# A fp32 decoder block on one core: low parts of the split weights first, one product split a tick later, and token roots spread through DRAM

## The chip, the cores and the metric

The kernel runs on one core of one Trainium2 chip. The metric is the device time of one execution in microseconds, lower is better; the figure of a kernel is the median of its runs.

## The reference, cut to what matters

One layer on 2048 tokens of width 1024, everything in float32:

```python
h = rms_norm(x, norm_g)                       # one root per token
u = h @ w_in                                  # 9728 columns: conv v, B, C, z; q, k, v, attn z; two gates
y_c = b_c * causal_depthwise_conv(c_c * v_c, conv_w) * silu(z_c)
y_a = y_c @ w_conv_out
q, k = rms_norm(q, q_norm_g), rms_norm(k, k_norm_g)
o = sliding_window_attention(q, k, v, sinks) * silu(z_a)   # window 128, blocks of 128, 16 heads on 4 kv heads
y_b = o @ w_attn_out
merged = g_a * y_a + g_b * y_b                # sigmoid gates
x + merged @ w_out
```

Almost all of the arithmetic is matrix products with 1024 on the contracted side.

## The kernel before

**Tiles and products.** The 2048 tokens are worked in two tiles of 1024 (`T`), each in two halves of 512 (`H`). A product of weights and activations is made from three TensorE passes: each operand is rounded to a "high" part by a copy on ScalarE (ACT), and the rest, the "low" part, is left by a subtraction on VectorE (DVE); TensorE (PE) then adds high·high, high·low and low·high. `product` (L467) issues these as 12 matmuls of 128x512: for each of four chunks two with the high weights and a third with the low ones.

**Units.** A unit is a block of 256 output columns for one tile. `sunit` (L486) computes it in a Strassen-like form with seven products in place of eight, in the order 1, 5, 6, 2, 7, 3, 4, on three PSUM banks called X, V and Y. Its weights come as pieces (`pieces_of`, L361): piece "a" (for products 1, 2), "d" (product 4), "sums" (additions and subtractions on the raw weights, four DVE steps of 128x512), then "s" (products 6 and 5) and "t" (products 3 and 7). Each of a, s and t is a high part of 128x1024 on ACT and a low part of 128x1024 on DVE; the names in the profile end in `_ah`/`_al`, `_sh`/`_sl`, `_th`/`_tl`. A ring of weight slots lets the s piece of the next unit be made only once product 3 of this one is through, so it has two products' time until product 5 of the next unit reads it.

**Ticks.** The order of the work is written by hand. `run` (L668) steps through the products; one step is a tick, some 2.7 us of TensorE. In each tick it issues, in this order: the product with what ends it (`fin`), the high part of one weight piece (`hi`), the first three functions that were put on this tick (`at`, filled by `put`), the low part (`lo`), the other functions, and four steps of the woven chains. `Woven` (L208) holds chains of small DVE steps, and slips one of them in behind each DVE instruction. Every engine works through its own instructions in the order in which they were issued; engines wait for each other by semaphores.

**What ends a product.** For the q units `fin_q` (L793) copies or adds the result to `qt`, splits it (`parts`, L832: `q_h` on ACT, `q_l` on DVE) and writes both to DRAM. For product 7 the result is a pair (Y, s5), which DVE adds; the ACT part waits for that add, and the DVE part for the ACT one. For the last z units (`za`), `fin_z` (L1192) multiplies by SiLU and hands the chunk to `use_y` (L1743), which, for the last two chunks, at once forms operands from it (`ca`, `form`: again a copy on ACT and a subtraction on DVE, `ophc` in the profile).

**Token roots.** RMSNorm's root of each token is computed with the tokens on the partitions (`rt`, `rtok`, four columns for a half). The activations are used with the tokens along the free axis, so the roots have to be spread over all partitions: `x_roots` (L598) makes four TensorE transposes of 128x128 into a PSUM bank (`ptr`), and one ACT copy to `rb`. For the first tile `turned` (L1513) does it on ticks 6 and 12 (`TURNED_AT`), while the k and v products run; for the second tile `roots` in `next_tile` (L1671) does it on ticks 9 and 17 of the first tile's last stage (`ya`, L1230), and `norm_l` (from tick 11) and `norm_r` (from tick 18) multiply by `rb` on DVE (`h<-h,cols,rb`). In the stage `ya` the SP queue carries the loads of gate values (`tha`, L1328) and weights.

Of the kernel before, what the change touches and what calls it, by code (L numbers as in the profile page):

```python
# [58 lines left out]
K_AT = (1, 1, 4)  # L59

T0_SHIFT = 1
TURNED_AT = (6, 12)

K_ROOT = True
CSUM_AT = (5, 8, 11, 14)
CONV_AT = (2, 2, 3, 3, 4, 4, 5, 5, 6, 6, 7, 7, 8, 8, 9, 9, 10, 10, 11, 11, 12, 12, 13, 13, 15, 15, 16, 16, 18, 18, 19, 19)
WO_AT = (29, 29, 30, 30, 31, 31, 32, 32)
# [24 lines left out]
def block_kernel(  # L92
# [51 lines left out]

    vd = dram.tile([NKV, HD, S // HD + 2, P], F32, name="vd")
    krd = [dram.tile([2, 2, T], F32, name=f"krd{t}") for t in range(NT)]
    od = [dram.tile([KC, P, T], F32, name=f"od{t}") for t in range(NT)]
    ocd = [dram.tile([KC, P, T], F32, name=f"ocd{t}") for t in range(NT)]
    yd = [dram.tile([KC, P, T], F32, name=f"yd{t}") for t in range(NT)]
# [4 lines left out]
    def hs(q):  # L154
        return slice(q * H, (q + 1) * H)
# [124 lines left out]
    def sub(o, a, b, eng=None):  # L280
        return (eng or vec).tensor_tensor(out=o, in0=a, in1=b, op=ALU.subtract)
# [23 lines left out]
    def added(n):  # L305

        if n not in summed_in:
            summed_in.add(n)
            raw = raws[2 * n + 1]
            if by_dma(plan[n][2]):  # L310
                nc.gpsimd.dma_start(raw[:, 0, 1], block_of(n, 1, 1), accum_op=ALU.add)
            else:
                return (lambda: add(raw[:, 0, 1], raw[:, 0, 1], raw[:, 1, 1]),)
        return ()
# [46 lines left out]
    def pieces_of(n):  # L361

        kind, srcs, key = plan[n]
        name = "w" + "_".join(str(i) for i in key)
        w = {}

        def two(hi, lo, src):
            return (lambda: nc.scalar.copy(hi, src),  # L370
                    lambda: vec.tensor_tensor(
                        out=lo, in0=src, in1=hi.bitcast(F32), op=ALU.subtract))

        if kind == "R":
            return w, []

        if kind in "SP":
            def pair(h, m1, m2, nm):
                hi, lo = (v.rearrange("p (i j c) -> p i j c", i=2, c=P) for v in wpair(f"{name}_{nm}"))
                for i, m in enumerate((m1, m2)):  # L380
                    w[m] = (hi[:, i], lo[:, i])
                raw = raws[2 * n]
                return two(hi, lo, raw[:, h] if summed else raw[:, :, h])

            summed = []

            if kind == "P":
                return w, [(2, 2 * h, lambda h=h: pair(h, (h, 0), (h, 1), f"p{h}")) for h in range(2)]

            def single():  # L390
                hl = wpool.tile([P, 2, KP, P], F32R, tag="w", name=f"{name}_d")
                w[4] = (hl[:, 0], hl[:, 1])
                return two(hl[:, 0], hl[:, 1], raws[2 * n + 1][:, 1, 1])

            def sums():
                raw = raws[2 * n]

                def f():
                    summed.append(vec.chain(
                        *added(n),  # L400
                        lambda: sub(raw[:, 0, 0], raw[:, 0, 1], raw[:, 0, 0]),
                        lambda: sub(raw[:, 1, 1], raw[:, 1, 1], raw[:, 0, 0]),
                        lambda: sub(raw[:, 1, 0], raw[:, 1, 0], raw[:, 0, 0])))

                return (lambda: None, f)

            def of_sums(*args):
                summed[0]()
                return pair(*args)

            return w, [(2, 0, lambda: pair(0, 1, 2, "a")), (1, 0, single), (0, 0, sums),
                       (2, 0, lambda: of_sums(0, 6, 5, "s")), (2, 2, lambda: of_sums(1, 3, 7, "t"))]

        def part(p):
            hi, lo = (v.rearrange("p (j c) -> p j c", c=UC) for v in wpair(f"{name}_{p}"))
            w[p] = (hi, lo)
            return two(hi, lo, raws[2 * n + p])

        return w, [(2, 0, lambda: part(0)), (2, 2, lambda: part(1))]
# [10 lines left out]
    def piece():  # L430

        if not todo and (len(ready) > used[0] or not open_prep()):
            return None
        n, i, cost, last, f = todo[0]
        need = [2 * n + i] if plan[n][0] in "TP" else [2 * n, 2 * n + 1][: 1 + min(i, 1)]
        if live[0] + cost > WRING or any(k not in raws for k in need):
            return None
        todo.pop(0)
        live[0] += cost
        rawlive[0] -= last  # L440
        return f()

    def force(n, m):

        while m not in ready[n]:
            ab = piece()
            assert ab is not None, (plan[n], m, live)
            for f in ab:
                f()

    def unit(key):
# [146 lines left out]
    def x_roots(t, q, rs):  # L598

        pt = mbank(f"ptr{t}_{q}")  # L600
        for b in range(HB):
            nc.tensor.transpose(pt[:, b, :], rs[:, b : b + 1].to_broadcast([P, P]), ident)
        rb = slot([P, H], F32, f"rb{t}_{q}")
        nc.scalar.copy(rb, pt.rearrange("p b q -> p (b q)"))
        return rb

    def gain(c):
        return cols[:, C_G + c : C_G + c + 1]

# [59 lines left out]
    def run(gen):  # L669
        while True:  # L670
            tick[0] += 1
            if next(gen, gen) is gen:
                tick[0] -= 1
                return
            ahead_loads()
            hi, lo = (piece() if tick[0] >= W_FROM else None) or (None, None)
            if hi:
                hi()

            fs = at.pop(tick[0], [])  # L680
            for f in fs[:3]:
                f()
            if lo:
                lo()
            for f in fs[3:]:
                f()
            vec.some(WOVEN)

# [10 lines left out]
    class KV:  # L699
# [20 lines left out]

        def values(self, n):
            rooted[n // 2]()
            for b in (2 * n, 2 * n + 1):
                v = slot([P, NKV, 2, HD], F32R, f"v0_{b}")
                src = self.banks[b][:, UC:].rearrange("p (j d) -> p j d", d=HD)
                r = rtok[:, b : b + 1]
                nc.scalar.activation(out=v[:, :, 0], in_=src, func=AF.Copy, scale=r)
                vec.scalar_tensor_tensor(
                    out=v[:, :, 1], in0=src, scalar=r, in1=v[:, :, 0].bitcast(F32),
                    op0=ALU.mult, op1=ALU.subtract)  # L730
                for e, half in enumerate(HALVES):
                    nc.gpsimd.dma_start(
                        vd[:, :, 2 * (b + 1) + e].rearrange("j k d -> k j d"),
                        v[half].bitcast(F32).rearrange("p j l d -> p j (l d)"))
# [58 lines left out]
    def fin_q(t, j):  # L793
# [4 lines left out]
        def fin(i, q, val):  # L798
            nm = f"q{t}_{j}_{i}_{q}"
            qt = slot([P, H], F32, f"{nm}_t")  # L800
            into(qt, val)

            wait = QWAIT if (t, j) == (0, 0) else 0
            if wait:
                put(tick[0] + wait, lambda: parts(i, q, qt))
            else:
                parts(i, q, qt)

            def sums():
                if by_pe:  # L810
                    pt = turn4(qt, f"pt{nm}")
                else:
                    pt = mbank(f"pt{nm}")
                    vec.transpose(out=pt.rearrange("p b q -> p (b q)"), in_=qt)
                sq = head_square(pt, nm)
                put(tick[0] + 1, lambda: reduce(sq))

            def reduce(sq):
                if by_pe:
                    head_reduce(sq, ss, 2 * i + q)  # L820
                else:
                    n = 2 * i + q
                    vec.tensor_reduce(
                        out=ss[:, n * 16 : (n + 1) * 16], in_=sq.rearrange("p (h d) -> p h d", d=32),
                        axis=AX.X, op=ALU.add)
                left[0] -= 1
                if left[0] == 0:
                    put(tick[0] + 1, rms)

            put(tick[0] + 1 + (wait if by_pe else TURN_WAIT), sums)  # L830
# [820 lines left out]
    def next_tile(t, n0):  # L1651
# [19 lines left out]
        def roots(q):  # L1671
            for b0 in (q * HB, q * HB + 2):
                seen_[b0]()
            st.setdefault("rb", {})[q] = x_roots(t, q, rt[q])

        rt, seen_ = {}, {}
        for b, n in enumerate((0, 1, 1, 2, 3, 4, 5, 6)):
# [3 lines left out]
        for g, n in enumerate((5, 6, 10, 11)):  # L1681
            put(n0 + n, lambda g=g: norm(2 * g))
            put(n0 + n + 1, lambda g=g: seen_[2 * g]())
        for q, n in enumerate((9, 17)):
            put(n0 + n, lambda q=q: roots(q))
        for c in range(KC):
            put(n0 + 6 + c // 2, lambda c=c: raw_load(t, 0, c, st))
# [18 lines left out]
    for t in range(NT):  # L1706
# [36 lines left out]
        def use_y(k, q, y):  # L1743
            att["raw"][k, q] = y
            if k >= KC - 2:
                ca(B_AT[k % 2, q], k // 2)

        zs = [("z", j) + fin_z(t, j, yd[t], "z", use_o) for j in range(NJ)]
        zs += [("za", j) + fin_z(t, j, od[t], "za", use_y) for j in range(NJ)]
# [141 lines left out]
```

## Time and profile before

| | |
|---|---|
| median of 3 runs | 1916.77 us (1916.73 to 1917.03) |
| the profiled execution | 1917.32 us, of which the profiled span is 1915.6 us |
| TensorE busy | 1904.0 us, 99% of the span, at full granted clock |
| VectorE busy | 1539.6 us, 80% |
| ScalarE busy | 991.7 us, 52% |
| GpSimd busy | 594.3 us, 31% |

How to read it: an instruction is named by its line, engine, operation and "out<-in" by the program's tiles. A row of waits has the engine that waited, then what it waited for, the total in microseconds, how many times, and the longest. In rows in order of time the first two numbers are the start and the duration in microseconds, and a note in brackets gives the idle time of the engine before the row and what ended it. A matmul of 128x512 is shown with 0.39 us though the next one starts 0.23 us after it, since matmuls overlap in the pipeline; so idle time that is shown for TensorE is smaller than what a wait costs.

### The profile page before, as it was taken

The page shows a single profiled execution, that of the slowest core. Times are in us where ns is not written, and L with a number is a line of the kernel's source. Part 1 is how long each engine was busy: PE and PEld are TensorE (multiplying, and loading weights), DVE is VectorE, ACT ScalarE, POOL GpSimd, SP SyncE. Part 2 cuts the span into 40 slices and gives each one's busy share as a digit, 9 for nine tenths or more (in the row PEclk, how much of TensorE's full clock was granted, in tenths as well). Part 3 has the DMA queues.
Part 4 walks back from the last instruction along what each step waited for, and adds up shares of the span by engine and source line. Part 5 has one row for each costly group of instructions (what it writes and reads, how often), then busy time and mean ns, then how long its engine had stood idle before and what let it go on. Part 6 is the DMA issues. An engine that isn't in the chain of part 4 may idle for free.

```text
span 1915.6 us, 27253 instructions
## 1 busy us (share of the span) xinstructions
PE 1904.0 (99%) x8718; PEld 1581.2 (83%) x8718; DVE 1539.6 (80%) x2614; ACT 991.7 (52%) x1969; POOL 594.3 (31%) x850
## 2 busy tenths in 40 slices
PE   9999999999999999999999999999999999999999
PEld 7788888888888888888878888888888888888887
DVE  7988899898878669669799888888998678777854
ACT  7665455456667344334565544556666335434321
POOL 2073425335565000011562333445555001021000
PEclk9999999999999999999999999999999999999999
DMA  8286455558787433894685554567776664698453
GB/s 293 79 235 190 152 159 175 170 175 248 235 254 231 151 108 137 300 282 94 184 216 152 175 159 141 166 208 246 236 242 210 230 232 160 232 262 203 154 174 112
DMA packets 209279, 371.79 MB, mean 194 GB/s; under 512 B 28592, under 2 KB 103344, under 8 KB 199152
## 3 DMA queue, kind: packets, MB, share of 16 engines
q1 hardware_dynamic: 174688, 281.63, 45.3%
q0 software_dynamic: 30848, 79.99, 16.1%
q10 hardware_dynamic: 3600, 8.42, 1.3%
q8 instruction: 69, 1.13, 0.3%
q14 instruction: 74, 0.61, 0.1%
HBM read 252.22 MB, written 117.72 MB: 193 GB/s over the span
## 4 chain that ended last, share of the span: by engine, by line
PE 54%; DVE 6%; issue 6%; POOL 2%; DMA 2%; ACT 0%; SPq 0%; POOLq 0%; DVEq 0%; ACTq 0%
PE Y L475 20%; PE ya L1238 4%; PE Vcv L475 2%; PE Vza L475 2%; PE Xza L475 2%; PE Vz L475 2%; PE Vo L475 2%; PE Xz L475 2%; PE Xo L475 2%; PE Xcv L475 2%; PE po L1100 1%; POOL q2d L840 1%; PE Vgb L475 1%; PE Qo L535 1%; PE Xgb L475 1%
## 5 line engine op out<-in xcount | busy, mean ns | idle before, releaser
L1062 POOL DMA_DIRECT2D x<-fd x256 | 139.5, 552 | 124.0 <-DMA fd<-f 66.9
L1035 ACT ACTIVATE p<-s,st,rq 128x128 f32<-128x128 f32 x256 | 112.8, 449 | 1.3 <-DMA fd<-f 1.3
L1083 POOL TENSOR_SCALAR_AFFINE_SELECT xh<-xh 64x512 fp32r<-64x512 f32 x64 | 65.0, 1015 | 145.8 <-DVE xl L243 108.8
L1055 POOL DMA_DIRECT2D fd<-f x64 | 36.9, 576 | 222.9 <-DVE f L243 207.0
L1334 POOL DMA_DIRECT2D mt<-tha x16 | 13.7, 859 | 257.6 <-DVE tha L243 231.4
L475 PE MATMUL Xcv<-oph,wcv_ah 128*128 128x512 f32 x256 | 79.2, 391 | 0.0
L1083 POOL TENSOR_SCALAR_AFFINE_SELECT xl<-xl 64x512 fp32r<-64x512 f32 x64 | 62.8, 981 | 4.4
L1083 POOL TENSOR_SCALAR_AFFINE_SELECT yp<-yp 64x512 fp32r<-64x512 f32 x64 | 57.7, 902 | 4.2
L1083 POOL TENSOR_SCALAR_AFFINE_SELECT yp<-xl 64x512 fp32r<-64x512 f32 x64 | 57.4, 896 | 3.1
L243 DVE TENSOR_TENSOR o<-po,o 64x256 f32<-64x256 f32 x128 | 53.4, 417 | 4.5 <-ACT o L1112 3.5
L475 PEld LDWEIGHTS Xcv<-oph,wcv_ah 128*128 128x128 f32 x256 | 47.6, 188 | 9.6
L370 ACT CAST wcv_sh<-wcv_raw 128x1024 fp32r<-128x1024 f32 x16 | 16.8, 1053 | 72.8 <-DVE wcv_raw L243 72.8
L243 DVE SCALAR_TENSOR_TENSOR y<-u,cols,y 128x512 f32<-128x512 f32 x64 | 50.5, 790 | 3.4 <-ACT y L1149 2.2
L1800 POOL DMA_DIRECT2D oc<-ocd x16 | 8.7, 542 | 142.7 <-DMA th<-gd 118.6
L274 ACT CAST ophc<-zain 128x512 fp32r<-128x512 f32 x64 | 37.3, 619 | 28.9 <-DVE zain L243 28.9
L840 POOL DMA_DIRECT2D q2d<-q_h x64 | 44.2, 691 | 22.9 <-ACT q_h L835 15.6
L1112 ACT COPY o<-po 64x256 f32<-64x256 f32 x128 | 47.0, 367 | 8.3 <-PE po L1100 4.3
L243 DVE TENSOR_TENSOR ophc<-zain,ophc 128x512 fp32r<-128x512 f32 x64 | 42.4, 688 | 11.1 <-ACT ophc L274 11.1
L243 DVE TENSOR_TENSOR p<-p,st 128x512 f32<-128x512 f32 x64 | 48.2, 753 | 3.2
L1035 ACT ACTIVATION_READ_ACCUMULATOR p<-s,st,rq 128x1 f32 x256 | 50.6, 198 | 0.0
L475 PE MATMUL Xcv<-oph,wcv_al 128*128 128x512 f32 x128 | 49.8, 389 | 0.0
L243 DVE STREAM_TRANSPOSE f<-p 128x512 f32<-128x512 f32 x64 | 45.5, 711 | 3.0 <-DVE p L243 0.2
(698 smaller groups left out, 6552.5 us busy)
## 6 DMA issues: line engine op xcount, KB each, us to landing
gd<-th SPq DMA_DIRECT2D x64, 256.0 KB, 3.0
wcv_raw<-in_w_units SPq DMA_DIRECT2D x16, 1024.0 KB, 5.6
q<-q2d SPq DMA_DIRECT2D x64, 256.0 KB, 5.0
v<-vd SPq DMA_DIRECT2D x128, 128.0 KB, 3.5
fd<-f POOLq DMA_DIRECT2D x64, 256.0 KB, 4.3
x<-fd POOLq DMA_DIRECT2D x256, 64.0 KB, 3.5
th<-gd SPq DMA_DIRECT2D x48, 256.0 KB, 5.6
wga_raw<-in_w_units SPq DMA_DIRECT2D x8, 1024.0 KB, 6.8
```

The source lines that it names most:

```text
L243: r = f(*args, **kw)
L274: nc.scalar.copy(hi, src)
L475: nc.tensor.matmul(ps, lhsT=w[:, j, :], rhs=b[:, m, :], start=start and j == 0 and i == 0, stop=j == KP - 1 and i == 2, skip_group_check=n ...
L535: nc.tensor.matmul(ps, lhsT=w[:, j, :], rhs=b[:, m, :], start=p == 0 and j == 0 and k == 0, stop=p == 1 and j == KP - 1 and k == 2)
L840: nc.gpsimd.dma_start(q2d[t][j][half, q * 2 * HB : (q + 1) * 2 * HB, i, e, :], src[HALVES[e]].bitcast(F32).rearrange("p (b x) -> p b x", x ...
L1035: nc.scalar.activation(out=p[:, i, :], in_=sg[:, i, HD : 3 * HD], func=AF.Exp, bias=st[:, 1, i : i + 1], scale=rv[:, i // 2, i % 2 : i % 2 ...
L1055: nc.gpsimd.dma_start(fd, f)
L1062: nc.gpsimd.dma_start(x[QUADS[k]], src[k])
L1083: nc.gpsimd.affine_select(out=d4, in_=s4, pattern=[[0, 2], [-32 * sg, 2], [0, G], [-sg, 32]], compare_op=ALU.is_gt if prev else ALU.is_ge, ...
L1100: nc.tensor.matmul(po[:, cs], lhsT=v2[:, kind, :], rhs=xx[:, :, h * HD : (h + 1) * HD], start=n == 0, stop=n == 2)
L1112: nc.scalar.copy(ov, pov[oth, :, e])
L1238: nc.tensor.matmul(ps, lhsT=w[:, j, cs], rhs=o[:, m, :], start=n == 0 and i == 0, stop=n == KC - 1 and i == 2)
```

## The change

Seven edits. (1) The s piece's low part is issued ahead of all functions of its tick (`LO_BEHIND`), the t piece's stays behind three. (2) The "sums" chain is cut in two, and the s piece forces only its first part (`SPLIT_SUMS`). (3) In q units the split of product 7's result is put one tick later (`PART_WAIT`). (4) For the last chunks of `za` the operands are formed one tick later (`USE_WAIT`). (5) In `KV.values` both high parts of v are issued ahead of both low parts (`V_WAIT` is 0 throughout). (6) The first tile's second spread of the roots is put on tick 11 in place of 12. (7) The second tile's roots are written by an SP DMA to a DRAM tensor, four bytes at a time, and read back by a second SP DMA to all partitions, on ticks 7 and 15 in place of 9 and 17; the eight transposes and two ACT copies go.

```diff
-TURNED_AT = (6, 12)
+TURNED_AT = (6, 11)
+SPLIT_SUMS = True
+PART_WAIT = ((0, 1), (0, 1))
+USE_WAIT = (1, 1)
+V_WAIT = (0, 0, 0, 0)
+LO_BEHIND = (0, 3)
+ROOTS_AT = (7, 15)
...
+    xrd = dram.tile([NT, T], F32, name="xrd")
...
                     summed.append(vec.chain(
-                        *added(n),
-                        lambda: sub(raw[:, 0, 0], raw[:, 0, 1], raw[:, 0, 0]),
+                        *added(n), lambda: sub(raw[:, 0, 0], raw[:, 0, 1], raw[:, 0, 0])))
+                    summed.append(vec.chain(
                         lambda: sub(raw[:, 1, 1], raw[:, 1, 1], raw[:, 0, 0]),
                         lambda: sub(raw[:, 1, 0], raw[:, 1, 0], raw[:, 0, 0])))
...
             def of_sums(*args):
+                if args[0] or not SPLIT_SUMS:
+                    summed[-1]()
                 summed[0]()
-                return pair(*args)
+                return (*pair(*args), LO_BEHIND[args[0]])
...
+    def x_roots_by_dram(t, q, rs):
+        nc.sync.dma_start(xrd[t, hs(q)].rearrange("(b p) -> p b", p=P), rs)
+        rb = slot([P, H], F32, f"rb{t}_{q}")
+        nc.sync.dma_start(rb, xrd[t, hs(q)].unsqueeze(0).to_broadcast([P, H]))
+        return rb
...
-            hi, lo = (piece() if tick[0] >= W_FROM else None) or (None, None)
+            hi, lo, *m = (piece() if tick[0] >= W_FROM else None) or (None, None)
...
-            for f in fs[:3]:
+            m = m[0] if m else 3
+            for f in fs[:m]:
                 f()
             if lo:
                 lo()
-            for f in fs[3:]:
+            for f in fs[m:]:
                 f()
...
                 nc.scalar.activation(out=v[:, :, 0], in_=src, func=AF.Copy, scale=r)
+                made.append((b, v, src, r))
+            if V_WAIT[n]:
+                put(tick[0] + V_WAIT[n], lambda: self.lows(made))
+            else:
+                self.lows(made)
...
-            wait = QWAIT if (t, j) == (0, 0) else 0
+            wait = QWAIT if (t, j) == (0, 0) else PART_WAIT[t][isinstance(val, tuple)]
...
-            st.setdefault("rb", {})[q] = x_roots(t, q, rt[q])
+            st.setdefault("rb", {})[q] = x_roots_by_dram(t, q, rt[q])
...
-        for q, n in enumerate((9, 17)):
+        for q, n in enumerate(ROOTS_AT):
...
-                ca(B_AT[k % 2, q], k // 2)
+                put(tick[0] + USE_WAIT[t], lambda: ca(B_AT[k % 2, q], k // 2)) if USE_WAIT[t] else ca(B_AT[k % 2, q], k // 2)
```

More of the change, by code (lines that the diff above doesn't have):

```diff
@@ L447, in force @@
             assert ab is not None, (plan[n], m, live)
-            for f in ab:
+            for f in ab[:2]:
                 f()
@@ L722, in values @@
             rooted[n // 2]()
+            made = []
             for b in (2 * n, 2 * n + 1):
@@ L727, in values, with lows @@
                 nc.scalar.activation(out=v[:, :, 0], in_=src, func=AF.Copy, scale=r)
+                made.append((b, v, src, r))
[3 more added lines that the diff above has]
+                self.lows(made)
+        def lows(self, made):
+            for b, v, src, r in made:
                 vec.scalar_tensor_tensor(
```

## The prediction, made before the changed kernel ran

> **What bounds the kernel now.** I read the page's busy times first, then the list of what TensorE waited for, then the rows in order of time around each of those waits.
>
> ```profile
> PE 1904.0 (99%) x8718; PEld 1581.2 (83%) x8718; DVE 1539.6 (80%) x2614; ACT 991.7 (52%) x1969; POOL 594.3 (31%) x850
> ```
>
> TensorE is idle for 1% of the span, some 12 us. No edit takes a product away, so the change can gain only eight transposes and a part of that idle time. What ended it, for TensorE over the whole span:
>
> ```profile
> PE Vq L475 <- DVE wq_sl L243: 1.1, 3, 0.4
> PE Y L475 <- DVE s5ya L243: 1.0, 1, 1.0
> PE Vcv L475 <- DVE wcv_sl L243: 0.9, 3, 0.3
> PE Y L475 <- DVE ophc L243: 0.7, 2, 0.4
> ```
> ```profile
> PE Vga L475 <- DVE wga_sl L243: 0.3, 1, 0.3
> ```
>
> The reader should see that VectorE is late each time, and that seven waits are for the s piece's low part (`_sl`). What one costs, from TensorE's rows at a q unit of the second tile:
>
> ```profile
> 971.90 0.62 PE L475 MATMUL Xq<-oph,wq_ah 128*128 128x512 f32 x2
> 972.36 0.39 PE L475 MATMUL Xq<-oph,wq_al 128*128 128x512 f32 x1
> 972.58 0.61 PE L475 MATMUL Vq<-oph,wq_sh 128*128 128x512 f32 x2
> 973.61 0.50 PE L475 MATMUL Vq<-oph,wq_sl 128*128 128x512 f32 x1 [0.41 <-DVE wq_sl L243]
> 973.95 0.63 PE L475 MATMUL Vq<-oph,wq_sh 128*128 128x512 f32 x2
> ```
>
> An undisturbed group of three takes 972.58 - 971.90 = 0.68 us, the one with the wait 973.95 - 972.58 = 1.37 us. So a wait shown with 0.41 costs 0.69: I add 0.28 us to each wait shown.
>
> **The change part by part: q units (split a tick later, s low part first).** VectorE's rows ahead of that wait:
>
> ```profile
> 967.75 0.75 DVE L243 SCALAR_TENSOR_TENSOR q_l<-q_t,gqk,q_h 128x512 fp32r<-128x512 f32 x1 [0.79 <-ACT q_h L835]
> 968.42 0.68 DVE L243 TENSOR_REDUCE qss<-ptq 128x16 f32<-128x512 f32 x1
> 969.02 2.74 DVE L243 TENSOR_TENSOR wq_raw<-wq_raw 128x512 f32<-128x512 f32 x4
> 971.68 0.74 DVE L243 SCALAR_TENSOR_TENSOR q_l<-q_t,gqk,q_h 128x512 fp32r<-128x512 f32 x1
> 972.34 1.22 DVE L243 TENSOR_TENSOR wq_sl<-wq_raw,wq_sh 128x1024 fp32r<-128x1024 f32 x1
> ```
>
> The first `q_l` is product 7's: VectorE has added, stands idle 0.79 us for ACT, and subtracts. Put a tick later and behind the low part, it frees VectorE from 966.96 (967.75 - 0.79) to 968.42, 1.46 us. The four sums then begin at 967.56, and `wq_sl` would end near 972.1 in place of 973.56; TensorE wanted it at 973.61 less the 0.69 lost, 972.92. So the wait goes, with 0.8 us to spare. The moved split still costs VectorE its 0.75 us and two DMAs on the POOL queue, now behind `wq_sl`; behind them wait a reduce and the small root steps, which nobody reads for many ticks. All three Vq waits: 1.1 + 3 x 0.28 = -1.9 us. One of the three Vcv waits is the first cv unit's s piece, made in the last q unit's tick 6 (the trace has the same rows there): 0.3 + 0.28 = -0.6 us.
>
> The other waits for an s piece look different, in VectorE's rows of the second tile:
>
> ```profile
> 1135.77 0.68 DVE L243 TENSOR_TENSOR y<-Vb,y 128x512 f32<-128x512 f32 x1
> 1136.37 1.21 DVE L243 TENSOR_TENSOR wcv_sl<-wcv_raw,wcv_sh 128x1024 fp32r<-128x1024 f32 x1
> ```
> ```profile
> 1540.30 1.29 DVE L243 TENSOR_TENSOR cr<-cr,cr 128x512 f32<-128x512 f32 x2
> 1541.50 1.22 DVE L243 TENSOR_TENSOR wza_sl<-wza_raw,wza_sh 128x1024 fp32r<-128x1024 f32 x1
> ```
>
> At 1136 only the product's own multiply stands right ahead of the low part, and that comes from `fin`, before the tick's functions: the edit moves nothing there. Two Vcv waits and the Vga one stay. At 1540 two functions' subtractions do stand ahead; they now come behind. That wait is too short for the list. With two or three such small ones I take -0.4 us; bounds 0 and -0.6.
>
> Cost of the low part first: the functions' DVE work (attention steps, above all) comes 1.2 us later (1136.37's 1.21) in the tick, and VectorE may stand idle until ACT's high part is ready. Where the trace has functions ahead, the high part was done before them, so idle time is rare. Attention has whole ticks between its steps; that is the cover, and if it is gone each late step costs up to 1.2 us. Bounds over both tiles 0 and +2.5 us (two such waits); I take +0.4.
>
> Cutting the sums chain in two changes the order only where the s piece has to force it. In the rows above all four steps stand together ahead of `wq_sl`, because the four woven steps at a tick's end pop both chains alike. I take 0. Where it is forced, two steps come later, a gain or a loss of 1.2 us on VectorE, bounds -0.4 to +0.4 us.
>
> **Operands of the last za chunks a tick later.** VectorE's waits from 1593 to 1606 us, the row of its work from 1604 to 1628, and the late operand itself:
>
> ```profile
> DVE ophc L243 <- ACT ophc L274: 3.7, 6, 0.7
> ```
> ```profile
> 1604.00:1628.00 24.00, 23.64 (x105) 19.26 (x104) 23.70 (x37) 11.89 (x20) 4.68 (x9) 1.00 0.49 169
> ```
> ```profile
> 1625.42 1.90 DVE L243 TENSOR_TENSOR ophc<-zain,ophc 128x512 fp32r<-128x512 f32 x3
> ```
>
> Multiply, copy on ACT, subtract: VectorE stands idle some 0.7 us in each, and four of the six are the ones that move. It then works without a pause (23.70 of 24 us) until the operand that TensorE waits for. Up to 2.7 us earlier, less what it must newly wait for TensorE's results on the way, is well over the 0.4 that is missing. First tile alike. The operands themselves come a tick later in order but not in time, as the queue ahead of them is shorter. Gain 0.7 + 2 x 0.28 = -1.3 us; bounds 0 and -1.3.
>
> **The second tile's roots by way of DRAM.** The transposes removed, in TensorE's rows and the tile's:
>
> ```profile
> 829.47 0.62 PE L1238 MATMUL ya<-opa,wya_1h 128*128 128x512 f32 x2
> 829.92 0.39 PE L1238 MATMUL ya<-opa,wya_1l 128*128 128x512 f32 x1
> 830.15 0.60 PE L602 MATMUL ptr<-ident,rt 128*128 128x128 f32 x4
> ```
> ```profile
> 831.05 0.40 PE L1238 MATMUL ya<-opa,wya_0l 128*128 128x512 f32 x1
> ```
> ```profile
> L602 PE MATMUL ptr<-ident,rt x8: 271/272/273, 830.1 to 852.7; 128*128 128x128 f32 x8
> ```
>
> From a group's first matmul to its third is 0.45 us (829.47 to 829.92); with the transposes ahead it is 0.90 (830.15 to 831.05). Two sets: -0.9 us. The Trainium skill, page "TensorE: Matmul & The Clock Gate", section "Part 4: PE-mode transpose", gives some 275 ns for a 128x128 transpose inside a kernel; eight by that would be 2.2 us (an estimate) and the sum 1.3 us lower. The trace agrees with it as a duration (272 ns) but not as a cost, because four of them pass in 0.45 us.
>
> What is added: two SP DMAs a half, in series, since the read waits on SP for the write to land. The trace has no write of four-byte pieces. The nearest rows are the k roots' own trip through DRAM, and a DMA that also has 512 packets:
>
> ```profile
> krb<-krd SPq DMA_DIRECT2D x8, 128.0 KB, 7.1
> ```
> ```profile
> krd<-krt SPq DMA_DIRECT2D x4, 4.0 KB, 2.3
> ```
> ```profile
> q2d<-q_h POOLq DMA_DIRECT2D x64, 128.0 KB, 4.0
> ```
> ```profile
> 838.51 0.75 DVE L243 SCALAR_TENSOR_TENSOR h<-h,cols,rb 128x512 f32<-128x512 f32 x1
> ```
> ```profile
> 827.08 0.17 DVE L596 COPY rt<-hr_r 128x2 f32<-128x2 f32 x1
> ```
> ```profile
> 844.47 8.94 SPq L1328 DMA_DIRECT2D tha<-gd  x4
> ```
> ```profile
> 842.07 0.17 DVE L596 COPY rt<-hr_r 128x2 f32<-128x2 f32 x1
> ```
> ```profile
> 855.89 0.74 DVE L243 SCALAR_TENSOR_TENSOR h<-h,cols,rb 128x512 f32<-128x512 f32 x1
> ```
>
> For the write I take 4.0 us (it has the packets of `q2d`; low end 2.3), for the read 7.1 us. Second half: roots ready 842.2; `tha` loads that stand before it in SP's order leave SP at some 845 (an estimate from the row at 844.47); 845 + 4.0 + 7.1 = 856.1 against a first use at 855.89. First half: ready at 827.2, and 827.2 + 11.1 = 838.3 against 838.51. Both come just in time; and ACT, which loses a copy and a wait for the transposes, runs ahead. SP stands in the wait 4 us a time; behind it are only the next `tha` loads, of which two come 8 us apart. I take 0; bounds -0.4 (ACT's head start cures a short wait late in `ya`) and, below, a rival.
>
> **First tile's second spread on tick 11.**
>
> ```profile
> 38.63 0.16 DVE L596 COPY rtok<-hr_r 128x4 f32<-128x4 f32 x1
> ```
> ```profile
> PE Qga L535 <- DVE oph L243: 0.5, 2, 0.2
> ```
> ```profile
> 40.34 0.60 PE L602 MATMUL ptr<-ident,rtok 128*128 128x128 f32 x4
> ```
>
> A tick is 2.72 us, so TensorE comes to the transposes at 37.6, but the roots are ready at 38.8: a new wait of 1.2 us. But in the next unit, `Qga`, TensorE waits for VectorE anyway, 0.5 + 2 x 0.28 = 1.1 us, and VectorE's own work there is not later for it, so the delay takes the place of that wait. Reordering v's two halves shifts VectorE by tenths. Together +0.2; bounds -0.5 and +1.2.
>
> **Sum.** -1.9 - 0.6 - 0.4 + 0.4 - 1.3 - 0.9 + 0.2 = -4.5 us. Against the profiled execution of 1917.32 (span 1915.6 and 1.7 around it) that is 1912.8; it stands 0.55 over the median 1916.77, so the forecast for the median is 1912.3 us, 0.23% less.
>
> **The rivals.** *Half of it is given back.* VectorE is the late engine everywhere; what it gains at the s piece it may owe at the next thing TensorE waits for (the Y bank's add, `s5ya` at 1.0 us, stays as it is), and the tick-11 wait may not be absorbed. With the ends +2.5 for late steps and +1.2 in place of 0.4 and 0.2 the sum is -1.4: 1915.4. For it: seven terms with little slack; against it: the rows show 0.8 us to spare in q units.
>
> *The roots are late (the other side).* VectorE waits at 855.89 with the rest of its work queued behind, and is nearly full from there on:
>
> ```profile
> 860.00:890.00 30.00, 29.88 (x133) 24.40 (x132) 27.75 (x44) 10.57 (x17) 4.06 (x6) 1.00 0.54 122
> ```
>
> Only 2.25 us are free in these 30. Each microsecond beyond that reaches TensorE, through gate products that free its PSUM banks. To lose the 4.5 gained and 3.8 more, the roots must land 2.25 + 8.3 = 10.6 us late, a trip of 22 us in place of 11: it decides only there, with 1920.6 us and more. The read's 7.1 us speaks for some lateness; no row near speaks for that much.
>
> *The roots are a few microseconds late.* A write of twice `q2d`'s time, 8 us, brings the second half's to 860.1, 4.2 us late; less the 2.25 free that is +2.0, 1914.3. For it: four-byte pieces, which no row has. Against it: only 2 KB move. The Trainium skill, page "DMA: Bandwidth & Descriptors", sections "Specifications" and "Bandwidth", has writes below 512 B as read-modify-write and some 10.5 ns a packet; 512 packets by that take 5.4 us (an estimate) beside its 2 us fixed. By that the write is 7.4 us, the roots 3.6 us late, the time some 1.4 us higher than forecast, 1913.7. No row here shows a packet of four bytes.
>
> *The splits do nothing.* If VectorE waits for ACT elsewhere instead, only transposes go: 1916.77 - 0.9 = 1915.9.
>
> **How the numbers follow.** 0.2% of 1916.77 is 3.8 us, about what a measurement of this kernel can tell from no change: faster means below 1912.9. Forecast 0.57; half given back 0.22, roots a few microseconds late 0.08 and splits that do nothing 0.06, all three within 0.2%; very late roots 0.07, slower. The range reaches from the forecast with the good ends of the bounds (another -0.2 for small waits, -0.4, -0.4, -0.7 gives 1910.6, rounded to 1910.0) to past the three middle rivals, 1916.5.
>
> **What would show it.** Right: no `wq_sl` and no `ophc` row among TensorE's waits, while two `wcv_sl`, one `wga_sl` and the `s5ya` row remain; no `ptr<-ident,rt`; `rb` landing by 839 and 857. Wrong: TensorE waits for `tha` or `oph` near 860 to 890, a `ptr<-ident,rtok` wait of a microsecond that is not given back at `Qga`, or new waits for attention's tiles (`po`, `s`).

## The result, and the profile after

The changed kernel takes 1922.91 us (median of 6 runs, 1922.43 to 1929.79) against 1916.70 for the kernel before on the same chip: a ratio of 1.0037, 95% interval 1.0026 to 1.0048. It is slower by some 6 us where 4.5 us less were forecast. The profiled execution of after took 1922.68 us, 5.4 more than the one of before (1917.32).

The busy times of after, and what TensorE waited for over its whole span:

```profile
PE 1902.5 (99%) x8710; PEld 1581.8 (82%) x8710; DVE 1539.3 (80%) x2614; ACT 989.4 (52%) x1967; POOL 589.9 (31%) x850
```
```profile
PE ya L1265 <- DVE tha L251: 7.0, 3, 4.3
PE s L1033 <- DMA q<-q2d: 2.4, 1, 2.4
...
PE ptr L612 <- DVE rtok L606: 1.4, 2, 1.1
PE Vcv L485 <- DVE wcv_sl L251: 0.7, 2, 0.3
...
PE Vga L485 <- DVE wga_sl L251: 0.3, 1, 0.3
```

The rows of `wq_sl`, `ophc`, `zs`, `s5ya` and `Qga` are gone, and two `wcv_sl` and one `wga_sl` are left, as forecast except for `s5ya`. With the prediction's 0.28 us added to each wait that went, that is 1.9 (`wq_sl`) + 0.5 (one `wcv_sl`) + 1.3 (`ophc`) + 0.7 (`zs`) + 1.3 (`s5ya`) + 1.1 (`Qga`), and with 0.9 for the transposes 7.7 us gained. Two rows at the top are new: in the stage `ya`, where the second tile's roots are used, and at one attention step of the first tile. The next rows show the first.

SP's and VectorE's rows of after around the two trips of the roots through DRAM, and the median time to landing of the two transfers (the last number, us):

```profile
828.02 0.37 SPq L619 DMA_DIRECT2D xrd<-rt  x1
837.82 0.32 SPq L621 DMA_DIRECT2D rb<-xrd  x1
838.24 1.56 SPq L1355 DMA_DIRECT2D tha<-gd  x2
...
849.69 0.37 SPq L619 DMA_DIRECT2D xrd<-rt  x1
861.09 0.32 SPq L621 DMA_DIRECT2D rb<-xrd  x1
```
```profile
845.92 0.75 DVE L251 SCALAR_TENSOR_TENSOR h<-h,cols,rb 128x512 f32<-128x512 f32 x1 [6.51 <-DMA rb<-xrd]
...
849.49 0.17 DVE L606 COPY rt<-hr_r 128x2 f32<-128x2 f32 x1
...
868.36 0.75 DVE L251 SCALAR_TENSOR_TENSOR h<-h,cols,rb 128x512 f32<-128x512 f32 x1 [6.85 <-DMA rb<-xrd]
```
```profile
rb<-xrd SPq DMA_DIRECT2D x2, 256.0 KB, 7.6
xrd<-rt SPq DMA_DIRECT2D x2, 2.0 KB, 10.6
```

SP issues the read when the write has landed: 837.82 - 828.02 = 9.8 us after the write, and 861.09 - 849.69 = 11.4 us, for 2 KB each time. With the read, VectorE gets the first roots 845.9 - 828.0 = 17.9 us after the write was issued and the second 18.7 us after. It stands still for 6.5 and 6.9 us. The reader should also see that the two halves are not independent: the second half's roots are ready at 849.5 in place of 842.1, because VectorE, which makes them, stood waiting for the first half's.

What TensorE makes of it, in its rows:

```profile
846.99 0.39 PE L1265 MATMUL ya<-opa,wya_1l 128*128 128x512 f32 x1
851.72 0.93 PE L1265 MATMUL ya<-opa,wya_0h 128*128 128x512 f32 x2 [4.34 <-DVE tha L251]
...
855.43 0.64 PE L1265 MATMUL ya<-opa,wya_0h 128*128 128x512 f32 x2
```

The wait costs 851.72 - 846.99 - 0.23 = 4.5 us. Behind it, nine matmuls take 855.43 - 851.72 = 3.71 us in place of nine times 0.23: they run at half speed, another 1.6 us. Two more waits for `tha` follow (2.7 us + 2 x 0.28), so the late roots cost 9.3 us here. The wait for `s` costs 2.7, the one for `rtok` 1.5 (1.2 more than before, + 0.28). 13.5 lost less 7.7 gained is +5.8, against the 5.4 by which the two profiled executions differ.

### The profile page after: what moved, and what is told of

Same layout as the page of the kernel before. It is cut to its first block, busy times and chain, and to the rows that moved or that the text cites. A ratio compares the mean times of both kernels' runs of the same rounds, so it can differ in the third digit from the quotient of the medians.

```text
span 1920.8 us, 27247 instructions
## 1 busy us (share of the span) xinstructions
PE 1902.5 (99%) x8710; PEld 1581.8 (82%) x8710; DVE 1539.3 (80%) x2614; ACT 989.4 (52%) x1967; POOL 589.9 (31%) x850
## 4 chain that ended last, share of the span: by engine, by line
PE 90%; DVE 5%; DMA 4%; issue 1%; ACT 0%; SPq 0%; POOL 0%; DVEq 0%; POOLq 0%
PE Y L485 33%; PE Vcv L485 4%; PE Xcv L485 4%; PE Xgb L485 2%; PE Vq L485 2%; PE Xq L485 2%; PE yb L1306 2%; PE Xza L485 2%; PE Vza L485 2%; PE po L1127 2%; PE Vgb L485 2%; PE Vz L485 2%; PE Xz L485 2%; PE Vga L485 2%; PE Vo L485 2%; PE Xo L485 2%
## 5 line engine op out<-in xcount | busy, mean ns | idle before, releaser
L1110 POOL TENSOR_SCALAR_AFFINE_SELECT xh<-xh 64x512 fp32r<-64x512 f32 x64 | 58.8, 919 | 150.3 <-DVE xl L251 114.9
L1361 POOL DMA_DIRECT2D mt<-tha x16 | 13.8, 860 | 265.8 <-DVE tha L251 251.2
L867 POOL DMA_DIRECT2D q2d<-q_l x64 | 44.1, 689 | 13.4 <-DMA q2d<-q_h 4.8
```

The costliest lines, as they stand in the source:

```text
L867: nc.gpsimd.dma_start(q2d[t][j][half, q * 2 * HB : (q + 1) * 2 * HB, i, e, :], src[HALVES[e]].bitcast(F32).rearrange("p (b x) -> p b x", x ...
L1110: nc.gpsimd.affine_select(out=d4, in_=s4, pattern=[[0, 2], [-32 * sg, 2], [0, G], [-sg, 32]], compare_op=ALU.is_gt if prev else ALU.is_ge, ...
L1361: nc.gpsimd.dma_start(mt[t][k, :, hs(q)], m, accum_op=ALU.add)
```

## The experiments

**The roots back on TensorE, and the roots alone.** First, all edits but the trip through DRAM; second, the trip alone on the kernel before.

```diff
-ROOTS_AT = (7, 15)
+ROOTS_AT = (9, 17)
-            st.setdefault("rb", {})[q] = x_roots_by_dram(t, q, rt[q])
+            st.setdefault("rb", {})[q] = x_roots(t, q, rt[q])
```

> The kernel after with one part undone: the second tile's roots go through TensorE transposes again, at ticks 9 and 17; every other edit stays. Theory A, the roots' trip through DRAM is late and alone causes the loss: 1912.2 to 1913.8 us (1916.8 - 4.5 + 0.9 = 1913.2), no wait of TensorE for tha, and two ptr<-ident,rt groups back. Rival B, the splits and the late steps cost the 6 us and the roots are harmless: 1919 us or more.

Measured: 1915.43 us (ratio to before 0.9991, 0.9982 to 1.0000). TensorE's waits:

```profile
PE s L1033 <- ACT p L1062: 2.3, 1, 2.3
```

7.5 us of the loss go with the roots; no wait for `tha` is listed. But 1915.4 is 1.6 us above the end of theory A's range, and the wait for `s` at 575 us is still there: the roots are not all.

The kernel before with the one part added:

```diff
-        for q, n in enumerate((9, 17)):
+        for q, n in enumerate((7, 15)):
...
-            st.setdefault("rb", {})[q] = x_roots(t, q, rt[q])
+            st.setdefault("rb", {})[q] = x_roots_by_dram(t, q, rt[q])
```

> The kernel before with one part added: the second tile's roots by way of DRAM at ticks 7 and 15, nothing else. Theory A: the roots cost all of what the change loses and the gain of the rest is missing, 1924 to 1927 us (1922.9 + 3.6 = 1926.5), with TensorE waiting for tha near 850. Rival B: 1915.5 to 1917.0, the two sets of transposes saved.

Measured: 1925.72 us (1.0044, 1.0031 to 1.0056), 9 us over before.

```profile
PE ya L1246 <- DVE tha L244: 8.6, 2, 6.8
...
PE Vq L476 <- DVE wq_sl L244: 1.1, 3, 0.4
```

The loss sits where it sat in after. Rival B falls in both.

**Is it the four-byte pieces?** VectorE turns the roots in blocks of 32x32, so that each DMA row has 32 tokens; the read stays.

```diff
-        nc.sync.dma_start(xrd[t, hs(q)].rearrange("(b p) -> p b", p=P), rs)
+        rr = small.tile([P, 32], F32, tag="sm", name=f"rr{t}_{q}")
+        vec.transpose(out=rr, in_=rs)
+        for i in range(4):
+            nc.sync.dma_start(
+                xrd[t, hs(q)].rearrange("(b i c) -> i b c", i=4, c=32)[i], rr[32 * i : 32 * i + HB])
```

> The kernel after, with the roots turned on VectorE and written to DRAM in 16 pieces of 128 bytes in place of 512 of four bytes; the same ticks, the same read. Theory A1, the write of 512 pieces is what is late: the write lands in 2 to 4 us, rb lands by 839 and 857, and the time is 1911.3 to 1913.3 us. Rival A2, two DMAs in series on a loaded queue are late whatever their pieces: rb still lands 5 us or more late and the time is 1919 us or more. In between (1914 to 1918): the pieces cause one part, the read another.

Measured: 1920.09 us, with a wide spread (1915.34 to 1922.23), ratio 1.0014, 1.0005 to 1.0023. SP's rows, and VectorE's first use of the second half's roots:

```profile
828.20 3.74 SPq L622 DMA_DIRECT2D xrd<-rr  x4
833.57 0.35 SPq L625 DMA_DIRECT2D rb<-xrd  x1
...
849.89 1.27 SPq L622 DMA_DIRECT2D xrd<-rr  x4
855.45 0.34 SPq L625 DMA_DIRECT2D rb<-xrd  x1
```
```profile
861.72 0.75 DVE L251 SCALAR_TENSOR_TENSOR h<-h,cols,rb 128x512 f32<-128x512 f32 x1 [2.25 <-DMA rb<-xrd]
```

The write is down to some 5.5 us and the trip to 861.72 - 849.89 = 11.8 us, nearly the 11.1 of the prediction. Yet TensorE waits 2.2 us for `tha` in the profiled execution, which is one of the fastest (1916.21 us); what the slower ones wait for is not shown. The second trip starts at 849.9, when I had taken 845. In this run the turning itself holds it up: the second half's roots are ready at 844.6, but the turn into `rr` stands behind six multiplies in VectorE's order and runs at 849.65. The median is in the range of rival A2, but its lateness of 5 us or more is not there in the profiled execution (2.25 us), and theory A1 does not hold either. So the pieces are one part of the cause, and the start is another.

**What do the writes do to the other transfers?** Roots through TensorE, and the four-byte writes issued too, read by nobody.

```diff
+            nc.sync.dma_start(xrd[t, hs(q)].rearrange("(b p) -> p b", p=P), rt[q])
+            st.setdefault("rb", {})[q] = x_roots(t, q, rt[q])
```

> The kernel after with the roots through TensorE transposes at ticks 9 and 17, and the two writes of 512 four-byte pieces issued too, which nobody reads. It prices what the writes do to the other transfers apart from the roots' lateness. Theory L, lateness of the roots is all: the time of the kernel with the roots back on TensorE, within 0.8 us. Rival D, the writes hold up the other DMAs (h and tha land late): 2 us or more above it.

Measured: 1918.19 us (1.0007, 0.9998 to 1.0016), 2.8 above the same kernel without the writes. The two windows in which the writes are under way, first without them and then with them (the last number is GB/s over all DMA, the one ahead of it the DMA engines' busy share):

```profile
838.00:850.00 12.00, 12.00 (x54) 9.95 (x53) 10.83 (x34) 2.63 (x3) 1.72 (x2) 1.00 0.88 264
861.00:873.00 12.00, 12.00 (x55) 9.94 (x54) 9.96 (x17) 3.96 (x6) 2.42 (x3) 1.00 0.86 227
```
```profile
838.00:850.00 12.00, 12.00 (x55) 9.94 (x54) 9.45 (x32) 1.06 (x1) 1.72 (x2) 1.00 1.02 177
861.00:873.00 12.00, 12.00 (x54) 9.95 (x53) 11.44 (x19) 2.40 (x5) 2.56 (x3) 1.00 0.98 157
```

The engines are busier and move about a third less: the small packets take time from all others. Transfers issued from 836 to 876 us land later, `h` after 9.2 us in place of 5.8 and the two weight loads after 13.2 and 13.4 in place of 9.7 and 8.6 (medians). TensorE waits 1.5 us for `tha` in this run, and the time is above the 2 us of rival D, so theory L falls. How much of the 2.8 us belongs to the writes is not shown: this run's wait at 575, long before them, was 3.4 us, 1.1 more than in the kernel without them, and the matmuls behind it ran at half speed for longer.

**Is it the buffer and the wait on SP, two ticks early?** The read and its buffer at ticks 9 and 17, the write at 7 and 15; once with 128-byte pieces and once with four-byte ones.

```diff
+        def roots_read(q):
+            st.setdefault("rb", {})[q] = x_roots_read(t, q)
...
+            put(n0 + n + 2, lambda q=q: roots_read(q))
```

> The kernel with the roots written in 128-byte pieces at ticks 7 and 15 (1920.1 us), and the read, with the buffer that it lands in, moved two ticks later, to where the transposes stood. Theory R, the buffer taken two ticks early and the read's wait on SP push the h and tha loads behind it: the wait of 2.2 us for tha goes, the roots land near 842 and 860 at the latest, and the time is 1914 to 1916 us with a narrow spread. Rival, any trip through DRAM is too late here: VectorE waits longer for rb than the 2.2 us that it did, and the time is 1920 us or more.

Measured: 1920.54 us (1916.84 to 1924.47), 1.0016, 1.0007 to 1.0025. No gain: VectorE waits 2.5 us for the first half's roots and 7.7 for the second's, where it had waited 2.2 in all. Theory R falls, the rival holds.

> The kernel after (four-byte pieces) with only the read and its buffer moved two ticks later. Theory R+D: the order of the buffers is mended, but the writes still hold up the other transfers and land some 10 us after their issue, so the time lies 2 to 4 us above that of the 128-byte pieces read later, and below 1922. Rival, the pieces are harmless once the read is later: within 1 us of it.

Measured: 1927.73 us (1.0056, 1.0042 to 1.0070), worse than after and above the 1922 that I had set as the limit, so neither expectation gave the time. A later read makes it later still; four-byte pieces cost 7 us more than 128-byte ones, not the 2 to 4 that I had expected.

**The wait at 575 us.** First three rows of before: the attention step `xl` on VectorE, ACT's exponentials, and the landing time of the store of `f` that these wait for.

```profile
562.00 0.69 DVE L243 TENSOR_TENSOR xl<-x,xh 128x512 fp32r<-128x512 f32 x1
```
```profile
572.38 0.46 ACT L1035 ACTIVATE p<-s,st,rq 128x128 f32<-128x128 f32 x1 [1.32 <-DMA fd<-f]
```
```profile
fd<-f POOLq DMA_DIRECT2D x1, 256.0 KB, 5.1
```

The rows of after that lead to the wait, engine by engine in order of time:

```profile
561.25 1.22 DVE L251 TENSOR_TENSOR wz_sl<-wz_raw,wz_sh 128x1024 fp32r<-128x1024 f32 x1
562.38 0.69 DVE L251 TENSOR_TENSOR xl<-x,xh 128x512 fp32r<-128x512 f32 x1
```
```profile
566.02 1.62 POOL L1110 TENSOR_SCALAR_AFFINE_SELECT xl<-xl 64x512 fp32r<-64x512 f32 x1
567.61 0.58 POOL L1082 DMA_DIRECT2D fd<-f  x1
```
```profile
fd<-f POOLq DMA_DIRECT2D x1, 256.0 KB, 7.7
```
```profile
575.36 0.46 ACT L1062 ACTIVATE p<-s,st,rq 128x128 f32<-128x128 f32 x1 [5.55 <-DMA fd<-f]
```
```profile
577.28 0.44 PE L1033 MATMUL s<-lows,kq 128*128 128x384 f32 x1 [2.44 <-DMA q<-q2d]
```

The s piece's low part now stands ahead of `xl`, an attention step. Behind `xl` POOL has its selects, and behind these the store of `f`. ACT's next exponentials wait for that store, 5.5 us in place of 1.3, and the list of the run with the roots back names `p` as what TensorE's `s` waits for. In after the row names a load of `q`, but ACT's last exponential ends at 577.23 there, 0.05 us before TensorE goes on. The store itself lands after 7.7 us in place of 5.1. Undone in the first tile's z units alone, with the roots on TensorE:

```diff
-                return (*pair(*args), LO_BEHIND[args[0]])
+                return (*pair(*args), 3 if key[:2] == ("z", 0) else LO_BEHIND[args[0]])
```

> The kernel with the roots back on TensorE (1915.4 us), and the s piece's low part again behind three functions in the first tile's z units alone. Theory Z, the low part put first delays attention's split of x there, POOL's selects and the store of f behind it, and so ACT's exponentials and TensorE's s at 575: that wait of 2.5 us goes, the old wait of 0.8 us at a z unit near 582 may come back, 1912.8 to 1913.8 us. Rival, the wait at 575 is a late transfer that has nothing to do with the low part: it stays and the time is 1915 to 1916.

Measured: 1911.82 us, ratio 0.9975, 0.9965 to 0.9985. It is faster than before and after, and 3.6 us below the same kernel with the low part first. The same rows:

```profile
560.87 0.68 DVE L251 TENSOR_TENSOR xl<-x,xh 128x512 fp32r<-128x512 f32 x1
561.47 1.22 DVE L251 TENSOR_TENSOR wz_sl<-wz_raw,wz_sh 128x1024 fp32r<-128x1024 f32 x1
```
```profile
566.04 0.58 POOL L1082 DMA_DIRECT2D fd<-f  x1
```
```profile
fd<-f POOLq DMA_DIRECT2D x1, 256.0 KB, 6.0
```
```profile
572.08 0.46 ACT L1062 ACTIVATE p<-s,st,rq 128x128 f32<-128x128 f32 x1 [2.15 <-DMA fd<-f]
```

Against these rows, `xl` of after starts 1.5 us later (0.4 of it because all of TensorE's work is that much later there), the store is issued 1.6 us later and takes 1.7 us longer to land, and ACT starts 3.3 us later. Why the store takes longer is not shown. The old wait near 582 did not come back in this run; in three of the five runs below, which have the same order in these units, it did (`zs`, 0.5 to 1.0 us). So this was the second cause, and the low part was it.

**The other edits, one at a time,** each undone in that 1911.8 us kernel. The kernel before took 1916.70 us on the chip of that kernel and of the next run, and 1917.19 us on the chip of all runs behind it; for these I take off the 0.5 us before I give a difference.

```diff
-TURNED_AT = (6, 11)
+TURNED_AT = (6, 12)
```

> The kernel with the roots on TensorE and the low part behind in the first tile's z units, and the first tile's second spread back on tick 12. Prices that edit alone. As the prediction has it, the wait of 1 us for rtok takes the place of the waits at Qga, worth 0.2 us: the time stays within 0.6 us of the same kernel with tick 11, and the Qga waits come back. Rival: the wait for rtok is a loss of its own, and the time falls by 0.9 us or more.

Measured: 1912.57 us (0.9975, 0.9965 to 0.9985), the same ratio, though the median is 0.75 us higher, a little more than the 0.6 expected; the `Qga` waits are back with 0.5 us in two. Tick 11 is worth nothing that these runs resolve, as the prediction had it.

```diff
-LO_BEHIND = (0, 3)
+LO_BEHIND = (3, 3)
```

> The same 1911.8 us kernel with the s piece's low part behind three functions in every unit. If the low part first is needed for the q units, the three Vq waits and the first Vcv wait come back at 0.69 us each in part or in whole, 1912.8 to 1914.3 us. Rival, the later split alone had freed VectorE: within 0.6 us of 1911.8, and the low part first had only a price.

Measured: 1912.40 us (0.9973, 0.9963 to 0.9983). No `wq_sl` wait came back; `s5ya` did:

```profile
PE Y L485 <- DVE s5ya L251: 1.0, 1, 1.0
```

The rival holds: the difference is 0.1 us, and the low part first was not needed at the q units. It brings nothing that these runs resolve in any other unit either.

```diff
-PART_WAIT = ((0, 1), (0, 1))
+PART_WAIT = ((0, 0), (0, 0))
```

> The same 1911.8 us kernel with the seventh product split in its own tick again. If the later split carries the gain at q units, the three Vq waits (0.69 us each) and the first Vcv wait come back: 1913.6 to 1914.4 us. Rival, the low part first is enough: within 0.6 us of 1911.8.

Measured: 1915.43 us (0.9990, 0.9981 to 0.9999), 3.1 more, and 3.0 more than the run ahead of it on the same chip.

```profile
PE Y L485 <- DVE zs L251: 1.0, 1, 1.0
PE Vcv L485 <- DVE wcv_sl L251: 1.0, 3, 0.3
...
PE Vq L485 <- DVE wq_sl L251: 0.8, 3, 0.4
```

The three Vq waits and the first Vcv wait are back. The later split is the edit that gains. These rows with 0.28 us a wait make 2.2 us, against the 2.5 that I had given it; the `zs` wait, which the run with tick 12 has too, can be the rest.

```diff
-USE_WAIT = (1, 1)
+USE_WAIT = (0, 0)
```

> The same 1911.8 us kernel with the operands of the last za chunks made in their own tick again. By the prediction the two waits for ophc come back, 1.3 us: 1912.8 to 1913.5. Rival, the other edits had already freed VectorE there: within 0.6 us.

Measured: 1912.90 us (0.9978, 0.9969 to 0.9988), 0.6 more, which these runs do not resolve. Both waits are back, 1.3 us with 0.28 for each:

```profile
PE Y L485 <- DVE ophc L251: 0.7, 2, 0.4
```

**Roots through DRAM that come in time.** 128-byte pieces, the second trip three ticks earlier than in after (on tick 12), and the left half's scaling one tick later. The edit is shown against the 1911.8 us kernel.

```diff
-ROOTS_AT = (9, 17)
+ROOTS_AT = (7, 12)
...
-            put(n0 + 11 + c // 2, lambda c=c: norm_l(t, c, st))
+            put(n0 + 12 + c // 2, lambda c=c: norm_l(t, c, st))
```

> The kernel with the low part behind in the first tile's z units (1911.8 us with TensorE roots), with the roots by way of DRAM in 128-byte pieces, the second trip started three ticks earlier (tick 12) and the left half's scaling a tick later, so that a trip of 11.7 us fits. Theory, lateness is what the trip costs: VectorE's wait for rb is under 1 us, no wait of TensorE for tha, and 1910.5 to 1912.3 us (1911.8 - 0.9 = 1910.9). Rival, the added transfers cost by themselves, through the loads of h and tha that they push back: 1914 us or more although the roots are on time.

Measured: 1911.54 us (0.9969, 0.9956 to 0.9981). SP's rows and VectorE's uses:

```profile
826.87 2.60 SPq L622 DMA_DIRECT2D xrd<-rr  x4
831.88 0.35 SPq L625 DMA_DIRECT2D rb<-xrd  x1
840.77 1.27 SPq L622 DMA_DIRECT2D xrd<-rr  x4
845.96 0.34 SPq L625 DMA_DIRECT2D rb<-xrd  x1
```
```profile
840.67 1.37 DVE L251 SCALAR_TENSOR_TENSOR h<-h,cols,rb 128x512 f32<-128x512 f32 x2
...
855.42 0.75 DVE L251 SCALAR_TENSOR_TENSOR h<-h,cols,rb 128x512 f32<-128x512 f32 x1
```

VectorE does not wait for either (the first use comes 13.8 and 14.7 us after the write is issued), TensorE's list has a single wait of 0.2 us for `tha`, and the loss is gone. With trips that are started this early, the way through DRAM costs nothing that these runs resolve. Whether it gains the 0.9 us of the transposes is not resolved either: 0.8 us less than the kernel with the transposes, and the intervals of the two overlap. Cutting the sums chain in two and the new order of v's halves were not tried by themselves.

## Why the prediction was wrong

**The step that failed: the roots by way of DRAM,** "For the write I take 4.0 us" and "I take 0". The write of 512 four-byte pieces took 9.8 and 11.4 us, not the 4.0 of a DMA with as many packets of 256 bytes; the read, 7.6 us, was near the 7.1 taken. The Trainium skill, page "DMA: Bandwidth & Descriptors", sections "Specifications", "Bandwidth" and, for the 2 us fixed, "Anatomy of one DMA", gave 7.4 us by the estimate in the prediction: nearer, and still short by 2.4 to 4.0 us. Undone, the step gives back 7.5 us; alone, it costs 9. With the measured medians, the prediction's own sum for late roots gives an estimate of 845 + 10.6 + 7.6 = 863.2, 7.3 us after the first use; less the 2.25 free that is +5.1, or 1917.4 us, already outside the range.

The rival "the roots are late" had the mechanism, and its 1920.6 us "and more" the time, but at 0.07, since it asked for a trip of 22 us. A trip of 18 us was enough, and two things left out of the step say why. First, I let the second half start at 845 whatever the first did; VectorE makes the second half's roots and stood in the first half's wait, so they came 7.4 us later (849.49 against 842.07; some 0.7 of it because all of the work is later there). Second, I looked for the damage behind 860, where VectorE has 2.25 us free; TensorE was hit at 847, by the first half already, and ran at half speed behind the wait.

**The second failure: "Attention has whole ticks between its steps; that is the cover".** I priced the late steps at 0.4 us, with 2.5 as the end. In the first tile's z units alone they cost 3.6 us (1915.43 against 1911.82). Of the 5.3 us between the two profiled executions (1916.14 and 1910.84), the wait at 575 makes 2.33 + 0.28 us and the half speed behind it another 1.7 (an estimate from the granted clock of 0.76 over 7 us). The cover was counted on VectorE alone. Behind `xl` stand POOL's selects, and behind these a store whose landing ACT waits for: a delay of 1.5 us of `xl` became 3.3 us at ACT. At the q units the prediction named what waits behind the moved split; here it did not do so for POOL.

**What was right.** The Vq waits and the first Vcv wait went, by the later split; the reading that it frees enough of VectorE's time there holds, but the low part first, which I had named together with it, adds nothing at q units. The two `ophc` waits went, and came back with 1.3 us, as forecast, when the edit was undone; in the time itself the 0.6 us is not resolved. Two Vcv waits and one Vga wait that stay: as forecast. The wait of a microsecond for `rtok` on tick 11 came and `Qga`'s went. `s5ya` was said to stay; in after it went, and in the runs above it comes and goes (0.6, none, 1.0 and 0.4 us); what decides it is not shown, and the rows of before alone could not carry a forecast of it.

Without the two failed steps the kernel is 4.9 us faster than before in the same comparison (1911.82 against 1916.70), where the sum without transposes had been -3.6. The range missed because one row was taken for a thing that it is not: its packets are as many, but not as small. The first half's lateness, the half speed and the second failed step did the rest.

## What to carry to other kernels

Price a DMA by the size of its pieces as well as their number, and if no row has that size, work the likeliest case out with the far end of the estimate too. When a result moves to a longer route, compare its earliest start, its trip and its first use for every half in turn, and carry the delay of one half into the start of the next. And ask for each step that is moved what stands in order behind it on every other engine: a step that VectorE can afford to do later may be what POOL waits for.

## What was not expected of the hardware

**Small writes slow all transfers.** 2 KB in four-byte pieces took 10.2 us (median of two) even when nobody read them, and while they were under way all DMA together moved 177 and 157 GB/s in place of 264 and 227.

**A wait of TensorE can cost more than its length.** In the run with the roots back, TensorE waited 2.33 us at 575, and its next matmuls ran at half speed:

```profile
577.56 0.69 PE L1033 MATMUL s<-lows,kq 128*128 128x384 f32 x1 [2.33 <-ACT p L1062]
...
579.17 1.11 PE L485 MATMUL Y<-oph,wz_th 128*128 128x512 f32 x2
...
581.35 0.63 PE L485 MATMUL Y<-oph,wz_th 128*128 128x512 f32 x2
```

The granted clock was 0.76 from 576 to 583 us there, and 0.57 in the run with the unread writes, whose wait was 3.4 us. In after the wait of 4.3 us brought it (the rows at 851.72), the one of 2.4 us at 574 did not: its next window shows 1.00. In the run with four-byte pieces and a later read, a wait of 2.8 us at 875 brought it (0.64 from 878 to 880 us) and one of 2.3 us at 577 did not. So at 2.3 to 2.8 us it may or may not happen, and in each of these runs at 3.4 us and more it did. The Trainium skill, page "TensorE: Matmul & The Clock Gate", section "Part 1: The HAM clock gate (the "warmup" mystery)", has the clock halved after an idle window of some 3.4 us, of a free-running counter, and given back after a busy one of that length. The half clock agrees. The slow stretch of matmuls fits that length here (some 3.5 us) and in after (3.7), but lasted some 5 us in the run with the unread writes; that a wait of 2.3 us was enough in one run does not agree with a full window of idle time. It also has a part in the wide spread of the kernels with late roots. With 128-byte pieces (1915.3 to 1922.2 us) the mean granted clock was 0.999 to 1.000 in the three executions up to 1916.3 us and 0.997 to 0.999 in the eight from 1918.7 us on. An estimate: 0.001 of 1920 us is 1.9 us, so up to 2 to 6 us of TensorE's time were lost to the clock there. How much else these executions waited is not shown.
